# State-space inputs and outputs reordered through DRAM, and one GELU operation per chunk, in a hybrid decoder block

## The chip, the cores and the metric

The program runs on one core of a Trainium2 chip. A core has a matrix engine (TensorE, PE in the profile, its weight loads PEld), a vector engine (VectorE, DVE), a scalar engine (ScalarE, ACT), GpSimd (POOL) and a synchronisation engine (SyncE, SP), which in the kernel before issues all transfers. Each engine works off its own instructions in order. The metric is device time in microseconds of one execution, lower is better.

## The reference, cut to what matters

One decoder layer on 512 tokens of width 1024 in float32: a conditioned norm, one input projection, two parallel token mixers (attention, and a state-space branch called S5), their gated merge, and a mixture of 32 experts. The change touches the S5 branch only:

```python
ug = u.reshape(B, S, 32, 16)                    # 512 columns = 32 groups of 16 channels
bu_re = einsum('bsgh,gph->bsgp', ug, bb_re)     # 64 states a group; bu_im alike
xr, xi = associative_scan(...)                  # x[t] = a * x[t-1] + bu[t], complex, along 512 tokens
y = einsum(xr, c_re) - einsum(xi, c_im) + d_skip * ug
y = gelu(y)                                     # then y @ w_glu, split, sigmoid gate
```

## The kernel before, in words

Weights come in 52 units of 512 KB (ws, four buffers). Of each, ACT makes a rounded copy wh (line 153) and VectorE the remainder wl (line 90), and PE multiplies three products (hh by wh, hl by wh, hh by wl; line 180, for v line 185). The input projection first makes u and two of the q blocks in six PSUM banks (line 543, acc), then the other q and the k blocks (acc), v (vps), and gates. Beside it PE computes the conditioning vector from 32 units adaw (line 749, mvb), which have two, later four buffers.

The S5 branch is worked in four chunks c of 128 channels and is interleaved with that projection: `tick` (line 788) advances a generator, `ssm_steps` (line 704). The scan is taken four tokens at a time. So the tokens t = 4b + q of a chunk, channels 32j + h, are brought into a tile U (us in the profile) whose partitions are 32q + h, with free dimensions j and b, in `ssm_u`: sixteen ACT copies of 32 partitions by 128 elements, with a step of 4 tokens on the reading side (line 420). They read u from PSUM for chunk 0, and for the others from a copy of u in SBUF (line 574). Then, for each chunk: `ssm_in` makes the input matrices W by PE transposes (bt, line 428) and ACT copies (line 429); `ssm_rotate` multiplies (bu, line 652) and VectorE rotates with cos and sin tables (m, z); `ssm_scan` scans; `ssm_back` rotates back (xri); `ssm_y` multiplies into one PSUM bank yp (lines 692 and 694), whose partitions are 32p + h, tokens t = 4b + p. Sixteen ACT operations apply the GELU and put each piece of 32x128 into its place in yf, with a step of 4 tokens on the writing side (line 698). ACT rounds yf to ygh and VectorE makes the rest, ygl; both are read much later, by the GLU. The table of chunk c + 1 (`table`, lines 409 to 411) needs two ACT table loads around it, since the GELU and the sine are in different sets.

The order of each engine's instructions in this part is chosen when the kernel is built, by the framework's scheduler with its own time line; only the first projection (lines 519 to 564) is in the order written. PSUM bank 4 holds yp of one chunk at a time, banks 2 and 3 hold bt and bu, U has two buffers, and yf has two (tag hf).

SP waits in order for what a transfer needs (a free buffer, the data, and a free one of eight completion counters taken in turn); what is queued behind it waits too.

Of the kernel before, what the change touches and what calls it, by code (L numbers as in the profile page):

```python
# [9 lines left out]
F32 = mybir.dt.float32  # L10
# [3 lines left out]
AF = mybir.ActivationFunctionType  # L14
OP = mybir.AluOpType
# [4 lines left out]
T, D = 512, 1024  # L20
# [37 lines left out]
def hybrid_block(ctx: ExitStack, tc: tile.TileContext, x, cols, cst, ada_a, ada_b, b_rows, bc_rows, lamv, relb,  # L58
                 onehot, units, rw, rb, bpad, cpad, w_ein, w_eout, out):
    nc = tc.nc  # L60
    V, S, G, TE = nc.vector, nc.scalar, nc.gpsimd, nc.tensor
# [3 lines left out]
    dram = ctx.enter_context(tc.tile_pool(name="dram", bufs=1, space=DRAM))  # L65

    def bank(i, shape=(128, 512), name=None):
        return psum.tile(list(shape), F32, tag=f"b{i}", name=name or f"bank{i}")
# [3 lines left out]
    late = p1.enter_context(tc.tile_pool(name="late", bufs=1))  # L72
# [4 lines left out]
    def t1(tag, shape, dt=F32, name=None):  # L77
        pool = late if tag[:-1] == "tmp" else mid if tag[:-1] in ("BT", "CT", "sgA", "xs") else early
        return pool.tile(list(shape), dt, tag=tag, name=name or tag)
# [3 lines left out]
    def emit(o, f):  # L83

        if kept[0] is None:
            return f()
        kept[0].append((0.1 + math.prod(o.shape[1:]) / 960, f))

    def tt(o, a, b, op, eng=None):
        return emit(o, lambda: (eng or V).tensor_tensor(o, a, b, op=op))  # L90
# [21 lines left out]
    def f32(a):  # L112
        return a.bitcast(F32)
# [82 lines left out]
    def two(i, name):  # L196
        if i == 0:
            return [bank(0, name=name), bank(1, name=name)]
        t = pair(name=name)
        return [t[:, 0], t[:, 1]]  # L200
# [114 lines left out]
    v, y, t = (st4[:, j] for j in range(3))  # L315
# [97 lines left out]
    U, W = {}, {}  # L413

    def ssm_u(c):

        U[c] = t1(f"v{c % 2}", [128, 4, 128], name="us")
        for j in range(4):
            for q in range(4):
                S.copy(U[c][32 * q:32 * q + 32, j], uT[c][32 * j:32 * j + 32, q::4])  # L420

    def ssm_w(c, ps):

# [95 lines left out]
    with tc.manual_schedule(engines={mybir.EngineType.PE, mybir.EngineType.DVE, mybir.EngineType.Activation}):  # L519
# [4 lines left out]
        acc = two(0, "acc0") + two(1, "acc2") + [bank(m, name=f"acc{m}") for m in (4, 5)]  # L524
# [11 lines left out]
        for k in range(KC):  # L536
            first, second = unit_parts(UNITS[k]) if k in UNITS else (lambda: None, ) * 2
            for n in range(3 * 6):

                m, w = (n // 2, n % 2) if n < 12 else (n - 12, 2)  # L540
                b = 6 * k + m
# [26 lines left out]
    for _ in setup:  # L568
        pass

    uT = [acc[0]]
    for c in range(1, 4):
        uT.append(t1(f"u{c}", [128, T]))
        S.copy(uT[c], acc[c])
        if c == 1:
            ssm_u(0)
    qT, kT, vt = [None] * 4, [None] * 4, [None] * 4

# [57 lines left out]
    ygh, ygl = [None] * 4, [None] * 4  # L636
# [3 lines left out]
    def ssm_in(c):  # L640
        if c:
            ssm_u(c)
            ps = pair((128, 2, 4, 128), "bt")
            ssm_w(c, [ps[:, ri] for ri in range(2)])
# [43 lines left out]
    def ssm_y(c, x_):  # L688
        yp = bank(4, (128, 4, 128), "yp")
        for j in range(4):  # L690
            for ri in range(2):
                TE.matmul(yp[:, j], CA[c // 2][ri][:, 4 * (c % 2) + j].rearrange("p q h -> p (q h)"), x_[:, ri, j], start=ri == 0,
                          stop=False)
            TE.matmul(yp[:, j], G_[c][:, j].rearrange("p q h -> p (q h)"), U[c][:, j], start=False, stop=True)
        f = late.tile([128, T], F32, tag="hf", bufs=2, name="yf")
        for j in range(4):
            for p in range(4):
                S.activation(f[32 * j:32 * j + 32, p::4], yp[32 * p:32 * p + 32, j], AF.Gelu_apprx_tanh)  # L698
        ygh[c] = t1(f"u{c}", [128, T], F32R, name=f"ygh{c}")
        ygl[c] = t1(f"cos{c}", [128, T], F32R, name=f"ygl{c}")  # L700
        S.copy(ygh[c], f)
        tt(ygl[c], f, f32(ygh[c]), OP.subtract)

    def ssm_steps():

        z, x_ = None, None
        for c in range(4):
            z = ssm_rotate(c)
            if c + 1 < 4:
                ssm_in(c + 1)  # L710
            yield
            ssm_scan(c, z)
            yield
            if c:
                ssm_y(c - 1, x_)
                bias_load(c - 1)
                yield
            x_ = ssm_back(c, z)
            yield
            if c == 0:  # L720
                for p in range(4):
                    for half in range(2):
                        powers(CA[half], c0, "c", p + 1, p, half, tx[1])
                        yield
                for half in range(2):
                    setup_g(c0, half)
                    yield
            if c + 1 < 4:
                table(c + 1)
                yield  # L730
        ssm_y(3, x_)
        bias_load(3)
        yield
# [236 lines left out]
    for i in range(4):  # L970
        m2s = []
        for m in (2 * i, 2 * i + 1):
# [5 lines left out]
            a = t1(f"u{m % 2}", [128, T], name="ma")  # L978
            b = t1(f"u{2 + m % 2}", [128, T], name="mb")
# [5 lines left out]
        for j in range(2):  # L985
            cs = slice(256 * i + 128 * j, 256 * i + 128 * j + 128)
            v = m2s[j].rearrange("p (i t) -> p i t", t=128)
# [238 lines left out]
    with tc.manual_schedule(engines={mybir.EngineType.PE}):  # L1226
# [10 lines left out]
        for i in range(NT):  # L1237
            ps = bank((5, 0, 1, 0)[i], name="po2")
            n = T if i < 3 else 256
            for s_ in range(KC * T // n):  # L1240
                k, c0 = s_ % KC, n * (s_ // KC)
# [19 lines left out]
    def slot(name, n=None, t=F32):  # L1261
        if n is None:
            n = nring[0] = nring[0] + 1
        return p2r.tile([128, 2, D], t, tag=f"r{FREED[n % RING]}", name=name)
# [110 lines left out]
    def act(hid):  # L1375
        a = p2.tile([128, 512], F32, tag="hT", name="sa")
        S.activation(a, hid[0], AF.Silu)  # L1377
        tt(a, a, hid[1], OP.mult)
        return a
# [94 lines left out]
    for p in range(NP - 1):  # L1474
# [7 lines left out]
        a = act(hid)  # L1482
# [65 lines left out]
    a = slot("sa", free[0] + 3)[:, 0, :512]  # L1548
# [265 lines left out]
```

## Time and profile before

| | |
|---|---|
| median of 3 runs | 939.51 us (938.96 to 942.91) |
| profiled execution | 938.94 us, span 937.1 us |
| PE busy | 893.2 us (95%) |
| DVE busy | 502.0 us (54%) |
| ACT busy | 300.3 us (32%) |
| transfers | 268.70 MB, mean 287 GB/s |

The span runs from the first to the last instruction of the profiled execution. A busy share is a mean over the whole span: the S5 branch lies between about 60 and 207 us, the attention part up to about 310, the merge, output projection and routing up to about 450, the experts after that. Waits are put down to the instruction that came last before the waiting one could start. PEclk is the granted clock of PE: 1.00 is 2.4 GHz, 0.50 is 1.2 GHz.

### The profile page before, as it was taken

Reading aid. Unit: us, or ns where it says so; the run is one execution under the profiler, and the core shown is the slowest. Engines: PE = TensorE matmul, PEld = TensorE weight load, DVE = VectorE, ACT = ScalarE, POOL = GpSimd, SP = SyncE. Lnnn points to the kernel's source line nnn. Section 1 sums busy time; section 2 is a strip of 40 time slices with the busy share of each in tenths; the row PEclk is TensorE's granted clock in tenths of the full one; section 3 lists DMA queues with packets and bytes.
Section 4 is the critical chain, followed back from the end, with each engine's and each line's share of the span. In section 5 each row is a group of like instructions: output and inputs, shape, how many; then the busy total and the mean of one; then the engine's idle time right before and its main releaser. Section 6 shows DMA issues by size and latency. Waiting matters only on the chain.

```text
span 937.1 us, 12889 instructions
## 1 busy us (share of the span) xinstructions
PE 893.2 (95%) x4967; PEld 554.4 (59%) x4967; DVE 502.0 (54%) x1256; ACT 300.3 (32%) x616; POOL 2.2 (0%) x8
## 2 busy tenths in 40 slices
PE   8997997889999999999999999999999999999994
PEld 4775765567778788778455543555435554355343
DVE  7896685656765557469524432544225442244336
ACT  4565568895644433243201000010000100001014
POOL 0000000000000000000000000000000000000000
PEclk9998999999999999999999999999999999999998
DMA  9925765612222623691899999999999999999952
GB/s 362 376 82 175 253 219 194 218 55 86 68 68 69 220 94 126 262 376 40 343 379 417 420 420 420 420 420 420 420 420 420 420 420 419 420 420 420 419 174 93
DMA packets 77590, 268.70 MB, mean 287 GB/s; under 512 B 5535, under 2 KB 11567, under 8 KB 77524
## 3 DMA queue, kind: packets, MB, share of 16 engines
q1 hardware_dynamic: 77524, 267.82, 72.9%
q8 instruction: 41, 0.67, 0.3%
q14 instruction: 25, 0.20, 0.1%
HBM read 265.68 MB, written 3.17 MB: 287 GB/s over the span
## 4 chain that ended last, share of the span: by engine, by line
PE 83%; ACT 6%; DVE 6%; DMA 3%; issue 1%; SPq 0%; DVEq 0%; ACTq 0%
PE hid L1412 23%; PE yb L1419 11%; PE acc L180 11%; PE cb L1397 7%; PE xg L1155 6%; PE pAS L180 5%; PE po L185 4%; PE acc L543 4%; DMA adaw<-ada_b 3%; ACT us L420 3%; PE plg L180 2%; ACT yf L698 2%; PE pv L864 1%; PE lp L1088 1%; PE mv L474 1%
## 5 line engine op out<-in xcount | busy, mean ns | idle before, releaser
L1412 PE MATMUL hid<-w,xT 128*64 128x512 f32 x1024 | 222.9, 592 | 0.0
L1412 PEld LDWEIGHTS hid<-w,xT 128*64 128x64 f32 x1024 | 73.3, 137 | 145.3 <-issue 136.5
L1419 PE MATMUL yb<-w,sa 128*64 128x512 f32 x480 | 106.3, 595 | 0.0
L90 DVE TENSOR_TENSOR sa<-sa,hid 128x512 f32<-128x512 f32 (+1 forms) x17 | 11.1, 656 | 166.3 <-PE hid L1412 153.9
L90 DVE TENSOR_TENSOR wl<-ws,wh 128x1024 fp32r<-128x1024 f32 x52 | 63.5, 1223 | 56.1 <-ACT wh L153 45.4
L90 DVE TENSOR_TENSOR x<-x,cb 128x512 f32<-128x512 f32 (+1 forms) x132 | 79.9, 664 | 2.0 <-PE cb L1397 2.0
L153 ACT ACTIVATE wh<-ws 128x1024 fp32r<-128x1024 f32 x51 | 53.7, 1057 | 80.0 <-PE acc L180 24.5
L180 PE MATMUL acc<-hh,wh 128*128 128x512 f32 x176 | 74.1, 421 | 4.4 <-ACT wh L153 4.4
L1390 ACT CAST yh<-yf 128x512 fp32r<-128x512 f32 x29 | 17.9, 619 | 172.0 <-DVE yf L96 141.7
L1419 PEld LDWEIGHTS yb<-w,sa 128*64 128x64 f32 x480 | 33.2, 137 | 65.0 <-issue 64.4
L180 PE MATMUL acc<-hl,wh 128*128 128x512 f32 x176 | 70.9, 403 | 0.0
L180 PE MATMUL acc<-hh,wl 128*128 128x512 f32 x176 | 70.6, 402 | 0.0
L1377 ACT ACTIVATE sa<-hid 128x512 f32<-128x512 f32 x15 | 9.0, 597 | 177.0 <-PE hid L1412 177.0
L96 DVE SCALAR_TENSOR_TENSOR yf<-yb,ws,gate 128x512 f32<-128x512 f32 x29 | 21.8, 751 | 80.8 <-PE yb L1419 80.3
L1155 PE MATMUL xg<-P,mh 128*128 128x256 f32 x224 | 54.7, 284 | 0.0
L1155 PE MATMUL xg<-P,ml 128*128 128x256 f32 x224 | 53.5, 280 | 0.0
L1397 PE MATMUL cb<-yh,PT 128*128 128x512 f32 x116 | 48.2, 416 | 0.4 <-ACT yh L1390 0.3
L1397 PE MATMUL cb<-yl,PT 128*128 128x512 f32 x116 | 45.9, 396 | 2.1 <-DVE yl L90 2.0
L1155 PEld LDWEIGHTS xg<-P,ml 128*128 128x128 f32 x224 | 42.2, 189 | 0.5
L1155 PEld LDWEIGHTS xg<-P,mh 128*128 128x128 f32 x224 | 42.1, 188 | 0.5
L180 PEld LDWEIGHTS acc<-hh,wh 128*128 128x128 f32 x176 | 33.7, 191 | 14.1 <-ACT wh L153 4.6
L180 PEld LDWEIGHTS acc<-hh,wl 128*128 128x128 f32 x176 | 33.5, 190 | 9.4 <-issue 1.6
(316 smaller groups left out, 1441.3 us busy)
## 6 DMA issues: line engine op xcount, KB each, us to landing
w<-w_ein SPq DMA_DIRECT2D x128, 1024.0 KB, 13.3
w<-w_eout SPq DMA_DIRECT2D x63, 1024.0 KB, 17.5
ws<-units SPq DMA_DIRECT2D x52, 512.0 KB, 3.6
adaw<-ada_b SPq DMA_DIRECT2D x32, 512.0 KB, 4.5
ada<-ada_a SPq DMA_DIRECT2D x8, 512.0 KB, 8.2
ada<-ada_a SPq DMA_DIRECT2D x16, 256.0 KB, 7.1
X<-x SPq DMA_DIRECT2D x4, 512.0 KB, 6.4
x<-x SPq DMA_DIRECT2D x4, 512.0 KB, 5.5
```

Of the source, the lines that this page charges most:

```text
L90: return emit(o, lambda: (eng or V).tensor_tensor(o, a, b, op=op))
L96: return emit(o, lambda: V.scalar_tensor_tensor(o, a, s, b, op0=op0, op1=op1, **k))
L153: return (lambda: S.activation(hi, st, AF.Copy) if u else V.tensor_copy(hi, st)), lambda: tt(lo, st, f32(hi), OP.subtract)
L180: TE.matmul(o, a, b, start=start and i == 0, stop=stop and i == 2)
L185: TE.matmul(o, a, b, start=start and i == 0, stop=stop and i == 2)
L420: S.copy(U[c][32 * q:32 * q + 32, j], uT[c][32 * j:32 * j + 32, q::4])
L543: TE.matmul(acc[m], (hi, lo, hi)[w], hT(k)[w // 2], start=k == 0 and n < 12 and w == 0, stop=k == KC - 1 and w == 2)
L698: S.activation(f[32 * j:32 * j + 32, p::4], yp[32 * p:32 * p + 32, j], AF.Gelu_apprx_tanh)
L1155: TE.matmul(o, (h2h, h2l)[w][i][:, 128 * k:128 * k + 128], P[:, i].rearrange("p a b -> p (a b)"), start=start, stop=i == NT - 1 and w == 1 ...
L1397: TE.matmul(ps, PT if len(y) == 2 else f32(PT), a, start=w == 0, stop=w == len(y) - 1)
L1412: m = TE.matmul(hid[q][64 * e:64 * e + 64], xT[p, k // 4][:, k % 4, 64 * e:64 * e + 64], ring[p][k][:, e, 512 * q:512 * q + 512], start=k ...
L1419: TE.matmul(yb[q][64 * e:64 * e + 64], hT_[:, f, 64 * e:64 * e + 64], ring[p][8 + f][:, e, 512 * q:512 * q + 512], start=f == 0, stop=f == ...
```

## The change

The reordering of u and of y is taken from ACT's small copies and given to transfers. For u, ACT copies a chunk from PSUM in one operation, with the tokens regrouped by q, and writes it to a DRAM tile ud from its own queue; four transfers from SP's queue read it back into U, one for each q, 64 KB each. For y, one GELU of 128x512 writes yf, a transfer from ACT's queue writes it to a DRAM tile yd, and four transfers on SP's queue read it into a second yf tile. The rounding cast and the subtraction then read that tile with a step of 128 elements between neighbouring tokens.

```diff
--- before.py
+++ after.py
@@ -415,9 +415,9 @@
     def ssm_u(c):
 
         U[c] = t1(f"v{c % 2}", [128, 4, 128], name="us")
-        for j in range(4):
-            for q in range(4):
-                S.copy(U[c][32 * q:32 * q + 32, j], uT[c][32 * j:32 * j + 32, q::4])
+        v = ud[c].rearrange("(j h) (q b) -> q h j b", h=32, b=128)
+        for q in range(4):
+            nc.sync.dma_start(U[c][32 * q:32 * q + 32], v[q])
 
     def ssm_w(c, ps):
 
@@ -568,11 +568,13 @@
     for _ in setup:
         pass
 
-    uT = [acc[0]]
-    for c in range(1, 4):
-        uT.append(t1(f"u{c}", [128, T]))
-        S.copy(uT[c], acc[c])
-        if c == 1:
+    ud = []
+    for c in range(4):
+        u_ = t1(f"u{c}", [128, T], name="u")
+        S.copy(u_.rearrange("p (q b) -> p q b", q=4), acc[c].rearrange("p (b q) -> p q b", q=4))
+        ud.append(dram.tile([128, T], F32, name=f"ud{c}"))
+        nc.scalar.dma_start(ud[c], u_)
+        if c == 0:
             ssm_u(0)
     qT, kT, vt = [None] * 4, [None] * 4, [None] * 4
 
@@ -693,13 +695,19 @@
                           stop=False)
             TE.matmul(yp[:, j], G_[c][:, j].rearrange("p q h -> p (q h)"), U[c][:, j], start=False, stop=True)
         f = late.tile([128, T], F32, tag="hf", bufs=2, name="yf")
+        S.activation(f, yp.rearrange("p j b -> p (j b)"), AF.Gelu_apprx_tanh)
+        yd = dram.tile([128, T], F32, name=f"yd{c}")
+        nc.scalar.dma_start(yd, f)
+        f = late.tile([128, T], F32, tag="hf", bufs=2, name="yf")
+        v = yd.rearrange("(p h) (j b) -> j h p b", h=32, b=128)
         for j in range(4):
-            for p in range(4):
-                S.activation(f[32 * j:32 * j + 32, p::4], yp[32 * p:32 * p + 32, j], AF.Gelu_apprx_tanh)
+            nc.sync.dma_start(f[32 * j:32 * j + 32].rearrange("h (p b) -> h p b", p=4), v[j])
         ygh[c] = t1(f"u{c}", [128, T], F32R, name=f"ygh{c}")
         ygl[c] = t1(f"cos{c}", [128, T], F32R, name=f"ygl{c}")
-        S.copy(ygh[c], f)
-        tt(ygl[c], f, f32(ygh[c]), OP.subtract)
+        f, yh, yl = (a.rearrange(o, **k) for a, o, k in ((f, "h (p b) -> h b p", dict(p=4)), (ygh[c], "h (b p) -> h b p", dict(p=4)),
+                                                         (ygl[c], "h (b p) -> h b p", dict(p=4))))
+        S.copy(yh, f)
+        tt(yl, f, f32(yh), OP.subtract)
 
     def ssm_steps():
```

The scheduler orders the instructions anew. On ACT, after the first projection (u copies and q copies, `us` is U, `lmt` a scalar of the attention, `tv` a bias table), before:

```order
L420 COPY us<-acc_281 32x128 x4
L574 COPY u_866<-acc_282 128x512
L420 COPY us<-acc_281 32x128 x12
L574 COPY u_885<-acc_283 128x512
L574 COPY u_887<-acc_283 128x512
L581 ACTIVATE q_889<-acc_284 128x512
L581 ACTIVATE q_891<-acc_285 128x512
L420 COPY us<-u_866 32x128 x6
L768 COPY tv<-tvp 4x320
L420 COPY us<-u_866 32x128 x10
L919 ACT_TABLE_LOAD
L919 ACTIVATE lmt<-lmt 128x2
```

The same place after the change:

```order
L574 COPY u<-acc_281 128x512
L574 COPY u<-acc_282 128x512
L576 DMA ud_868<-u 128x512
L576 DMA ud_877<-u 128x512
L574 COPY u<-acc_283 128x512 x2
L583 ACTIVATE q_887<-acc_284 128x512
L583 ACTIVATE q_889<-acc_285 128x512
L576 DMA ud_881<-u 128x512
L576 DMA ud_885<-u 128x512
L776 COPY tv<-tvp 4x320
L927 ACT_TABLE_LOAD
L927 ACTIVATE lmt<-lmt 128x2
```

The 32 small copies of chunks 0 and 1 are gone from in front of tv and lmt; four whole copies and four DMA issues stand there.

On SP, at the weight loads ws that follow the first projection, before:

```order
L747 DMA adaw<-ada_b 128x1024 x2
L145 DMA ws_917<-units 128x1024
L145 DMA ws_1027<-units 128x1024
L770 DMA tvd<-tv 4x640
L747 DMA adaw<-ada_b 128x1024 x2
L145 DMA ws_1110<-units 128x1024
```

The same place after:

```order
L755 DMA adaw<-ada_b 128x1024 x2
L420 DMA us<-ud_868 32x4x128 x4
L420 DMA us<-ud_877 32x4x128 x4
L145 DMA ws_915<-units 128x1024
L145 DMA ws_1013<-units 128x1024
L778 DMA tvd<-tv 4x640
L755 DMA adaw<-ada_b 128x1024 x2
L145 DMA ws_1096<-units 128x1024
```

Eight reads of us for chunks 0 and 1 now stand between the adaw loads and the two ws loads; each group of four waits for a write from ACT's queue.

On ACT, around the GELU of chunk 0 (`sin` and `tabtmp` belong to the next chunk's table), before:

```order
L420 COPY us<-u_885 32x128 x16
L698 ACT_TABLE_LOAD
L698 ACTIVATE yf<-yp 32x128 x16
L153 ACTIVATE wh_1847<-ws_1845 128x1024
L409 ACT_TABLE_LOAD
L409 ACTIVATE sin_1650<-tabtmp 128x512
L701 CAST ygh_1590<-yf 128x512
L410 ACTIVATE tabtmp<-tabtmp 128x512
```

And after:

```order
L429 COPY W<-bt 128x512 x2
L698 ACT_TABLE_LOAD
L698 ACTIVATE yf<-yp 128x512
L700 DMA yd_1549<-yf 128x512
L153 ACTIVATE wh_1793<-ws_1791 128x1024
L409 ACT_TABLE_LOAD
L409 ACTIVATE sin_1616<-tabtmp 128x512
L410 ACTIVATE tabtmp<-tabtmp 128x512
L709 CAST ygh_1556<-yf 128x512
L411 ACTIVATE cos_1615<-tabtmp,halfpi 128x512
```

The copies of us for chunk 2 are gone, the GELU is one operation with a DMA issue behind it, and the cast ygh has moved behind the table's second operation.

On SP, where chunk 2 is read and chunk 0 comes back, after (before, there are none of these reads):

```order
L755 DMA adaw<-ada_b 128x1024
L420 DMA us<-ud_881 32x4x128 x3
L755 DMA adaw<-ada_b 128x1024
L420 DMA us<-ud_881 32x4x128
L704 DMA yf<-yd_1549 32x4x128 x4
L145 DMA ws_2106<-units 128x1024
L755 DMA adaw<-ada_b 128x1024
L763 DMA mrd<-mr 4x256
```

The reads of us for chunk 2 and of yf for chunk 0 stand among the adaw loads, ahead of the next ws.

## Rows read from the trace of the kernel before

**Rows 1.** Table of stretches, core 0: us, busy us of each engine, PEclk, DMA share, GB/s.

```profile
75.50:86.10 10.60, 4.93 (x24) 2.73 (x21) 7.92 (x16) 5.83 (x10) 0.00 (x0) 0.68 0.46 162
86.10:143.20 57.10, 54.13 (x348) 39.79 (x347) 44.22 (x83) 32.92 (x70) 0.00 (x0) 1.00 0.69 238
143.20:156.80 13.60, 8.46 (x75) 6.10 (x73) 6.62 (x10) 10.52 (x20) 0.00 (x0) 1.00 0.38 120
156.80:174.30 17.50, 13.39 (x85) 9.34 (x83) 10.78 (x17) 16.78 (x37) 0.00 (x0) 0.92 0.65 237
182.60:198.20 15.60, 12.39 (x87) 8.18 (x85) 11.91 (x19) 14.89 (x31) 0.00 (x0) 1.00 0.43 167
207.00:310.00 103.00, 103.00 (x506) 81.73 (x505) 65.49 (x218) 54.52 (x125) 0.00 (x0) 1.00 0.23 73
500.00:880.00 380.00, 380.00 (x1965) 185.83 (x1964) 143.99 (x279) 34.10 (x66) 0.00 (x0) 1.00 1.03 420
```

**Rows 2.** List of waits, PE, 60 to 210 us: us in total, times, longest us.

```profile
PE acc L180 <- ACT wh L153: 4.4, 1, 4.4
PE bu L652 <- ACT W L429: 4.1, 1, 4.1
PE bt L428 <- DVE m L90: 3.6, 2, 2.3
PE sc L837 <- DVE qs L90: 3.2, 2, 2.8
PE mvb L749 <- DMA adaw<-ada_b: 2.9, 3, 1.5
PE yp L692 <- ACT yf L698: 1.6, 1, 1.6
PE mvb L749 <- DVE mr L90: 1.3, 1, 1.3
```

**Rows 3.** Instructions in order of time, ACT: start us, us, line, operation, count.

```profile
72.30 4.30 ACT L420 COPY us<-u 32x128 f32<-32x128 f32 x10
76.62 1.28 ACT L919 ACT_TABLE_LOAD   x1
...
78.81 2.00 ACT L153 ACTIVATE wh<-ws 128x1024 fp32r<-128x1024 f32 x2
...
132.94 6.93 ACT L420 COPY us<-u 32x128 f32<-32x128 f32 x16 [0.53 <-PE yp L694]
```

**Rows 4.** Instructions in order of time, PE, then DVE (its own view): wait in brackets.

```profile
79.91 0.79 PE L180 MATMUL acc<-hh,wh 128*128 128x512 f32 x1 [4.36 <-ACT wh L153]
...
78.15 0.16 DVE L96 SCALAR_TENSOR_TENSOR lmt<-lmt 128x1 f32<-128x1 f32 x1 [7.22 <-ACT lmt L919]
```

**Rows 5.** Groups of instructions by shape, ACT, 60 to 330 us: busy, mean ns, idle before.

```profile
L698 ACT ACTIVATE yf<-yp 32x128 f32<-32x128 f32 x64 | 25.1, 392 | 3.1 <-PE yp L694 2.4
...
L633 ACT ACTIVATE th<-acc 128x512 f32<-128x512 f32 x16 | 9.3, 580 | 0.0
```

**Rows 6.** Line 420: ns min/median/max, first and last start us, shape.

```profile
L420 ACT COPY us<-u x48: 408/418/447, 69.3 to 163.6; 32x128 f32<-32x128 f32 x48
L420 ACT COPY us<-acc x16: 252/256/260, 62.5 to 67.1; 32x128 f32<-32x128 f32 x16
```

**Rows 7.** Line 145 (weight loads): ns min/median/max of an issue; then issue to landing.

```profile
L145 SPq DMA_DIRECT2D ws<-units x52: 327/328/5805, 4.3 to 383.8; - x52
...
DMA to landing us min/median/max: 3.4/3.6/17.9
```

**Rows 8.** Transfer issues by line: count, KB each, median us from issue to landing.

```profile
adaw<-ada_b SPq DMA_DIRECT2D x32, 512.0 KB, 4.5
...
out<-fo SPq DMA_DIRECT2D x4, 512.0 KB, 2.6
...
B<-bsd SPq DMA_DIRECT2D x4, 256.0 KB, 3.8
...
colt<-cols SPq DMA_DIRECT2D x1, 107.5 KB, 2.0
```


## Prediction

> **What bounds the kernel now.** I read the table of stretches first. In its last two rows [rows 1] TensorE (PE) is busy all the time at a granted clock of 1.00, in the attention part (207 to 310 us) and in the expert part (500 to 880 us); the expert part also keeps the transfers full at 420 GB/s. So nothing is to be won there, and a microsecond won earlier reaches the end only if the expert weights start earlier too (a rival below). The lost time lies between 75 and 198 us, where PE's busy time is clearly below the stretch: 10.60 − 4.93 = 5.7 us idle in the first row, 13.60 − 8.46 = 5.1 in the third, 17.50 − 13.39 = 4.1 in the fourth, 15.60 − 12.39 = 3.2 in the fifth, and 57.10 − 54.13 = 3.0 spread over the long second one [rows 1]. After a wait PE also runs at the lower clock level: the first stretch has a mean of 0.68, so two thirds of it passed at 1.2 GHz, and about half of its 4.9 us of work, 2.5 us, is lost to that. The fourth has 0.92, 16% of 17.5 us at the low level, which costs 1.4 us.
>
> Then the list of waits says whom PE waits for [rows 2]: ScalarE's weight copy wh (4.4), its copy W (4.1) and its GELU yf (1.6); VectorE's m (3.6), mr (1.3) and qs (3.2); a transfer of adaw (2.9). ScalarE (ACT) is the root of more of it than its own rows. Its in-order timeline [rows 3] shows why: ten copies of us run from 72.30 for 4.30 us, and only at 78.81 come the two wh. PE's row of 79.91 has waited 4.36 us for the first of them [rows 4], since 75.5. VectorE sits behind the same queue: its row of 78.15 has waited 7.22 us for ACT's lmt [rows 4]. At 132.94 sixteen copies for chunk 2 take 6.93 us [rows 3], and the GELU of a chunk follows them. By group, ACT spends 25.1 us on 64 GELU pieces (6.3 a chunk) [rows 5], and on 64 copies 48 × 0.42 + 16 × 0.256 = 24.3 us [rows 6], 49.4 us in all.
>
> **The change part by part.** *Removed:* 64 copies and 64 GELU pieces, 49.4 us of ACT. *Added on ACT:* four whole GELUs of 128x512. The trace has none of that shape; a tanh of that shape from PSUM took 580 ns [rows 5], so 4 × 0.6. One more whole copy of u (0.6; three were there already). Eight transfer issues, which the trace shows on SP's queue only, at 0.33 us undisturbed [rows 7], so 8 × 0.33 = 2.6. ACT is relieved of about 44 us, some 11 per chunk.
>
> *The first wait (75.5 to 86.1).* u and the two q copies now come first on ACT, and lmt and wh stand right behind them, so ACT is ready for wh from about 72. What decides is when its weights arrive: the two loads ws now stand on SP's queue behind eight reads of us, and those behind ACT's writes. My reckoning: ACT starts on u at 62.5, as the first copy from acc did [rows 6]; six whole operations of 0.6 and four issues of 0.33 later, at 67.4, the last write is issued, and a write lands 2.6 us after its issue (the nearest row is the output of 512 KB [rows 8]), so 70.0. The first load goes out behind it near 70.2 (SP's order, and it takes over the completion counter of that write), lands 3.6 us later [rows 7], 74, and the cast (2.00 us for two [rows 3]) is ready at 75. PE wants it at 75.5. The second is ready about 1 us later. VectorE, free of its 7.22 us wait, has the other operand by 76.5. So the idle 5.7 and the clock loss 2.5 go, and I charge 0.5 for the tie: −7.7. Bounds: −8.2 if the loads land sooner; −4 if they land 4 us later, as a 256 KB read took 3.8 where I take 2.0 [rows 8].
>
> By the Trainium skill, *DMA: Bandwidth & Descriptors*, section "Issuing engines are not separate DMA queues", ACT's transfers run on the same 16 engines as SP's and interleave with them. The trace before cannot show it: all its program transfers are SP's. By that rule the four writes, 1 MB, would delay the two loads by 1 MB over 420 GB/s [rows 1], 2.5 us, and the sum would be about 2 us higher, inside my range.
>
> *The stretches 143.2 to 156.8 and 156.8 to 174.3.* Their idle 5.1 and 4.1 us, and 1.4 us of clock, come from PE waiting for yf, W, m and mr, each of which stands behind ACT's 13 us of pieces. After the change the yp bank is free 0.6 us after its last matmul, W and the weight copies follow at once, and us arrives by transfer while PE still multiplies v. What is late next is ACT's cast ygh, which now waits for the GELU's round trip: issue 0.33, write 2.6, four read issues 1.3, landing 2.0 (the nearest row, 107.5 KB alone [rows 8]) to 3.8, together 6.2 to 8.0 us. Ahead of that cast stand wh (1.0, half of 2.00), a table load (1.28 [rows 3]), sin and abs (0.58 each, as the tanh), 3.4 us, so ACT holds for 3 to 4.5 us. It saved about 12 in that chunk (6.9 + 6.3 − 0.6 − 0.3); behind the cast wait cos and the next wh, which PE needs a unit of v later, 24 passes of about 0.2 us (506 in 103 us [rows 1]). I cost the hold at nothing, hidden by that unit; if the cover is gone it costs up to 4.5 for each of chunks 0 and 1, 9 in all. The casts of chunks 2 and 3 stand behind work of the attention part. The sum takes −10.6 (5.1 + 4.1 + 1.4).
>
> *The rest.* The 3.2 us wait for qs hangs on VectorE's own chain of chunk 3, which keeps its length: 0, between −3.2 and +4 (if PE arrives ahead of VectorE). The 2.9 us for adaw stay, and a faster PE comes nearer to loads that need 4.5 us [rows 8] and are issued only when PE has freed their buffer: +0.5, between −2.9 and +6. The cast and the subtraction now read f with a stride. A small copy from PSUM takes 256 ns, from u in SBUF 418 [rows 6]; if all of that is the stride, it is 1.3 ns an element, 0.65 us on each of eight operations, beside work of other engines: 0, at most +5.
>
> Sum: −7.7 − 10.6 + 0.5 = −17.8 us. The profiled execution took 938.94 us, 0.6 below the median of 939.51, so 921.1 on its own scale; I predict **921 us**.
>
> **The rivals.** *A, only the first wait goes.* The holds at ygh and SP's queue (the reads of us wait there for PE's yp, those of yf for the write, with adaw and ws behind them) put back what the later stretches gave. For it: SP issues in order, and one load here took 17.9 us to land and 5.8 to issue behind a large transfer [rows 7]. Against it: the reads stand where SP waited for PE before too. 938.9 − 7.7 = **931 us**.
>
> *B, slower.* One mechanism: the read of yf back from DRAM gets stuck behind the adaw loads, ACT stops at ygh, and wh behind it starves PE. It decides once the round trip exceeds what ACT saved plus what stands ahead: 12 + 3.4 = 15.4 us. If landing takes the worst row, 17.9 us [rows 7], the round trip is 0.33 + 2.6 + 1.3 + 17.9 = 22.1, 6.7 us beyond that point. Chunks 0 and 1 then cost 13.4 us more than before instead of giving 10.6, while the first wait still goes: 938.9 − 7.7 + 13.4 = 944.6, **945 us**. Against it: that 17.9 stood behind a 1 MB transfer that is made once.
>
> *C, no change at the end.* The time is won but the expert weights do not start earlier, and with transfers full at 420 GB/s [rows 1] PE waits there instead: **939 us**. For it: share 1.03 from 500 to 880. Against it: PE is busy 380 of 380 us there, so the loads keep up, and they start when earlier buffers come free, which moves with PE.
>
> *D, it does not do what it says:* the whole GELU or the casts cost so much more that ACT is not relieved. With 44 us to lose I give it no time of its own and count it with C.
>
> **How the numbers follow.** Forecast 0.74, A 0.14, B 0.07, C with D 0.05. The forecast's own range is 914 to 929: at the low end all idle time of 75 to 198 us goes (5.7 + 3.0 + 5.1 + 4.1 + 3.2 = 21.1) and both clock losses (3.9), 938.9 − 25.0; at the high end the first wait gives only 4 and adaw takes 4 more than charged: 921.1 + 3.7 + 4. The range of 8 in 10 goes on to A, and below by 3 us, since gaps between matmuls too short to show as idle may close as well: 911 to 932. About 0.5% (4.7 us) is what a measurement of this kernel can tell from no change. Faster by more than that: 0.74 + 0.14 = 0.88; the same, C and D: 0.05; slower, B: 0.07.
>
> **What would show it.** Right: PE's row of the first weight pass after gp has no wait over 1 us; no row of PE waits for yf; VectorE no longer waits 7 us for lmt; the first score matmul, whose wait for qs ended at about 197 us before, starts between 175 and 183; everything from there on keeps its length. ACT's wait ahead of each ygh is 3 to 5 us, and its weight casts behind do not stand at the head of PE's waits. Wrong: the wait for wh stays with a transfer of ws as the releaser; PE waits for wh behind ygh; adaw heads PE's waits with over 8 us; or the expert part grows by what was won.

## The result and the profile after

The changed kernel took 926.99 us (median of 4 runs, 923.54 to 928.20), the kernel before in the same series 940.28 (938.96 to 942.91): ratio 0.9849, 95% interval 0.9814 to 0.9884. That is 13.3 us faster, where 18 were forecast: inside the range, 6 us from its likeliest value. The profiled execution took 926.62 us, its span is 924.8, where it was 937.1.

I cut both traces at the same points of the work. The *front* runs from the last matmul of the first projection to the first matmul of v (line 185). The *middle* runs from there to the first score matmul (line 837 before, 845 after). First the table of stretches of the kernel before (columns as in [rows 1]): front, middle, and a stretch behind the first score matmul:

```profile
63.59:120.94 57.35, 50.75 (x334) 36.60 (x335) 42.13 (x89) 32.92 (x71) 0.00 (x0) 0.94 0.62 215
120.94:197.03 76.09, 61.94 (x444) 43.55 (x442) 53.29 (x91) 64.57 (x132) 0.00 (x0) 0.98 0.55 196
198.80:202.30 3.50, 3.50 (x10) 2.75 (x9) 2.02 (x8) 3.40 (x9) 0.00 (x0) 0.51 0.44 150
```

And of the kernel after: front, in it the place of the first wait, middle, attention, and a part of the experts that is as long as the last row of [rows 1]:

```profile
64.61:120.98 56.37, 53.63 (x345) 37.59 (x345) 45.02 (x96) 24.17 (x46) 0.00 (x0) 0.94 0.80 271
76.95:86.40 9.45, 6.71 (x23) 3.95 (x23) 8.84 (x13) 3.17 (x3) 0.00 (x0) 0.65 0.68 239
120.98:186.56 65.58, 61.02 (x434) 43.49 (x432) 53.78 (x85) 34.39 (x51) 0.00 (x0) 0.97 0.73 240
186.56:298.00 111.44, 111.44 (x545) 88.44 (x544) 69.41 (x230) 59.29 (x133) 0.00 (x0) 1.00 0.25 78
488.00:868.00 380.00, 380.00 (x1964) 185.81 (x1964) 143.94 (x280) 33.96 (x66) 0.00 (x0) 1.00 1.03 420
```

The first length on a row tells it. The front is 57.35 before and 56.37 after: it gave 1.0 us. The middle is 76.09 and 65.58: it gave 10.5, of which 9.6 is idle time of PE (76.09 − 61.94 = 14.15 before, 65.58 − 61.02 = 4.56 after); the other 0.9 is work that moved, since eight adaw matmuls and two small ones now stand ahead of the first v matmul. From the first score matmul to the end it was 937.1 − 197.03 = 740.1 and is 924.8 − 186.56 = 738.2, another 1.8. Nearly all of that is the lower clock behind the wait for qs (0.51 in the third row, 1.7 us lost), which the kernel after does not have there. Against this stands 1.0 us ahead of the front (63.59 to 64.61), where the clock from 15 to 20 us is 0.67, and 1.00 before. Each engine does the same operations in both programs there, and of the kernels below some show the lower clock and some do not. Together −12.3, the difference of the spans. Attention and experts run as before: PE busy throughout at a clock of 1.00, the experts' transfers at 420 GB/s.

The list of waits of PE, 60 to 210 us, answers to [rows 2]:

```profile
PE mvb L757 <- DMA adaw<-ada_b: 3.1, 3, 1.3
PE yp L694 <- DVE xri L90: 2.5, 1, 2.5
PE acc L180 <- ACT wh L153: 1.7, 2, 1.2
```

The waits for yf, W, m, mr and qs are gone. The wait for wh, 4.4 us before, is 1.7 and did not go, and a new one, for xri of the last chunk, takes the place of the one for qs. ACT's groups by shape, 60 to 330 us, answer to [rows 5]:

```profile
L709 ACT CAST ygh<-yf 128x512 fp32r<-128x512 f32 x4 | 4.4, 1100 | 3.8 <-DMA yf<-yd 3.8
...
L698 ACT ACTIVATE yf<-yp 128x512 f32<-128x512 f32 x4 | 2.4, 600 | 5.6 <-PE yp L696 5.6
```

A whole GELU takes 600 ns, four of them 2.4 us in place of 25.1.

The first wait is read in order of time. SP's issues (start, length, line, transfer, count), first the two weight loads before the change, then the same place after it:

```profile
65.12 0.84 SPq L145 DMA_DIRECT2D ws<-units  x2
```

```profile
65.24 0.83 SPq L755 DMA_DIRECT2D adaw<-ada_b  x2
66.20 6.80 SPq L420 DMA_DIRECT2D us<-ud  x8
73.10 0.85 SPq L145 DMA_DIRECT2D ws<-units  x2
```

ACT, in order of time, at that place and around the first two round trips of y (the write yd, and the cast that waits for its reads):

```profile
77.04 1.06 ACT L153 ACTIVATE wh<-ws 128x1024 fp32r<-128x1024 f32 x1 [3.92 <-DMA ws<-units]
78.28 1.06 ACT L153 ACTIVATE wh<-ws 128x1024 fp32r<-128x1024 f32 x1 [0.19 <-DMA ws<-units]
...
132.73 0.33 ACTq L700 DMA_DIRECT2D yd<-yf  x1
...
141.66 1.09 ACT L709 CAST ygh<-yf 128x512 fp32r<-128x512 f32 x1 [3.21 <-DMA yf<-yd]
...
150.03 0.33 ACTq L700 DMA_DIRECT2D yd<-yf  x1
...
164.62 1.09 ACT L709 CAST ygh<-yf 128x512 fp32r<-128x512 f32 x1 [0.58 <-DMA yf<-yd]
```

Eight reads keep SP for 6.8 us; the two weight loads behind them leave at 73.10, ACT now waits for them instead of they for ACT, and PE, ready at 76.95, waits 1.18 and 0.52 us:

```profile
78.14 0.50 PE L180 MATMUL acc<-hh,wh 128*128 128x512 f32 x1 [1.18 <-ACT wh L153]
...
79.39 0.50 PE L180 MATMUL acc<-hh,wh 128*128 128x512 f32 x1 [0.52 <-ACT wh L153]
```

The round trip of chunk 0 is 132.73 to 141.66, 8.9 us. That of chunk 1 is longer, 150.03 to 164.62, 14.6 us, but other work and waits of ACT cover all of it but 0.58.

### The profile page after: what moved, and what is told of

Read it like the earlier page. It is cut to its first block, busy times and chain, and to the rows that moved or that the text cites. A ratio compares the mean times of both kernels' runs of the same rounds, so it can differ in the third digit from the quotient of the medians.

```text
span 924.8 us, 12835 instructions
## 1 busy us (share of the span) xinstructions
PE 895.0 (97%) x4967; PEld 554.8 (60%) x4967; DVE 504.1 (55%) x1256; ACT 256.5 (28%) x493; POOL 2.2 (0%) x8
## 4 chain that ended last, share of the span: by engine, by line
PE 86%; DVE 7%; DMA 4%; ACT 1%; issue 1%; SPq 0%; DVEq 0%; ACTq 0%
PE hid L1420 24%; PE acc L180 13%; PE yb L1427 11%; PE cb L1405 7%; PE xg L1163 6%; PE pAS L180 5%; PE po L185 4%; PE acc L543 3%; PE plg L180 2%; DMA adaw<-ada_b 1%; DMA yd<-yf 1%; PE pv L872 1%; PE lp L1096 1%; PE mv L474 1%; PE mvb L757 1%
## 5 line engine op out<-in xcount | busy, mean ns | idle before, releaser
L90 DVE TENSOR_TENSOR sa<-sa,hid 128x512 f32<-128x512 f32 (+1 forms) x17 | 11.1, 657 | 166.3 <-PE hid L1420 153.9
```

## The experiments

All times are medians of 4 to 6 runs against the kernel before in the same series; an interval of a ratio is ±0.2 to 0.35%, 2 to 3 us. So only differences above some 4 us can be told by the times, and the traces decide on mechanisms. A trace is of one execution, and that is not always a middling one: for u alone through SP it took 925.4 us (median 927.4), for y alone 928.7 (932.9), for the first SP experiment 930.5 (928.2), and for the two kernels without the hold 934.6 (930.0) and 929.8 (927.0). In the tables, "idle" is a stretch less PE's busy time, "clock" the sum over half-microsecond pieces of busy time × (1 − granted clock).

My first theory (T): ACT's relief is the gain, and the front gave its share back because SP issues in order. Rivals: the gain is the GELU's alone (G); the transfers, not the order, made the weights late (B).

**One part alone.** First the u part with the 16 GELU pieces a chunk kept (the main lines of the edit, seen from the changed kernel):

```diff
-        S.activation(f, yp.rearrange("p j b -> p (j b)"), AF.Gelu_apprx_tanh)
...
+                S.activation(f[32 * j:32 * j + 32, p::4], yp[32 * p:32 * p + 32, j], AF.Gelu_apprx_tanh)
```

> The u part of the change alone: us by transfers through DRAM, the GELU of a chunk in 16 pieces as before and no y transfers. ScalarE loses 24 us of copies and keeps 25 us of pieces. Theory T (what pays is ScalarE's relief in the stretch from 121 us to the first score matmul, which came 10.5 us earlier, and either half of the relief empties most of the queue): ratio to before about 0.991, 931 to 933 us; TensorE's wait for W (4.1 before) under 1 us, its wait for yf near 1 to 2 us again, first score matmul near 190. Rival G (the gain is the GELU's alone): 937 to 941 us.

Then the y part with the 64 copies kept (the copy of u from PSUM goes back to the old form as well):

```diff
-        for q in range(4):
-            nc.sync.dma_start(U[c][32 * q:32 * q + 32], v[q])
+        for j in range(4):
+            for q in range(4):
+                S.copy(U[c][32 * q:32 * q + 32, j], uT[c][32 * j:32 * j + 32, q::4])
```

> The y part of the change alone: one GELU per chunk and its way through DRAM, us by 64 copies on ScalarE as before. Theory T: the first wait is as long as before (4.4 us for wh near 75.5), since the copies stand ahead of it, but that wait was worth only about 2 us net; the later stretch gains most of its 10.5: 930 to 933 us, ratio about 0.991. Rival G (the gain is the GELU's alone): 926 to 928 us. Rival U (the gain is that of the copies alone): 937 to 941 us.

Measured: u alone 927.42 us (0.9874, interval 0.9852 to 0.9896), y alone 932.86 (0.9929, 0.9905 to 0.9952). The second is as T said, and its list of waits of PE has the first wait as before:

```profile
PE acc L180 <- ACT wh L153: 4.4, 1, 4.4
```

The first is 3.6 us below T's range: within what the times can tell, the u part alone gives all that the whole change gives. Its front, and its middle:

```profile
63.47:118.36 54.89, 52.59 (x345) 36.96 (x345) 44.83 (x96) 24.14 (x46) 0.00 (x0) 0.97 0.81 280
118.36:181.90 63.54, 58.76 (x433) 41.66 (x432) 49.25 (x82) 47.69 (x93) 0.00 (x0) 1.00 0.65 220
```

Both are shorter than in the changed kernel (56.4 and 65.6); behind the first score matmul it takes 3.5 us more (741.7 for 738.2), 1.7 of it lost to the lower clock. So in this order of work the y part adds nothing to the u part. G falls, and so does the rival U of the second text, by which y alone would have given nothing.

**SP's queue.** The reads of us issued by GpSimd, and, in another kernel, two weight loads (of the units 7 and 8) asked for earlier:

```diff
-            nc.sync.dma_start(U[c][32 * q:32 * q + 32], v[q])
+            nc.gpsimd.dma_start(U[c][32 * q:32 * q + 32], v[q])
```

> The changed kernel with the 16 reads of us issued by GpSimd instead of SyncE; the bytes and the writes are the same. Theory T (the first wait came back because SyncE issues in order and spent 6.8 us on eight reads, 66.20 to 73.10, so that the two weight loads left 8 us later than before): the two loads leave by 67.5, their casts stand at 73 to 74, the waits of 1.18 and 0.52 us at 78 go, and part of the 2.5 us lost at the lower clock with them: 922 to 925.5 us. Rival B (the loads were late because 2 MB of writes and adaw loads were on the same 16 transfer engines): the loads leave earlier but land no earlier than 76, and the time stays at 926 to 928 us. Either way us must be there by 74.3; if GpSimd's issue is slow, TensorE waits for us instead and the time is over 928.

```diff
+    load(7)
+    load(8)
     ud = []
```

> The changed kernel with the loads of weight units 7 and 8 asked for ahead of the copies of u, so that they stand ahead of the eight reads on SyncE. Theory T: no wait for wh at 78; the reads of us come 1 to 2 us later and TensorE, which has weights, multiplies q meanwhile: 922 to 926 us. Rival B: the bytes only change places, us lands 2.5 us later, TensorE waits for bu's operand or VectorE's chain of chunk 0 is late by that: 926 to 930 us.

Measured: 928.20 us (0.9867, 0.9844 to 0.9889) and 929.05 (0.9884, 0.9863 to 0.9905): no gain, and 2.7 and 3.1 us above T's ranges. The second is where B put it, yet without a wait for wh in a front of 53.6 us, as T had it. But it does not test the order alone, since its loads left long before the writes of u, as the last two of four that start at 41.17:

```profile
41.17 8.53 SPq L145 DMA_DIRECT2D ws<-units  x4
```

They were out of the crowded time altogether. The middle of the second is 70.3 us, with 4.7 of PE's waits for xri. The stretches of the first, front and middle, show that T was right on the front's length and blind to what follows:

```profile
64.85:118.05 53.20, 50.38 (x345) 35.96 (x346) 45.05 (x96) 24.38 (x47) 4.46 (x8) 1.00 0.82 287
118.05:189.79 71.74, 64.86 (x434) 45.90 (x432) 53.55 (x85) 34.21 (x50) 4.40 (x8) 0.91 0.69 226
```

The front is 3.2 us shorter than in the changed kernel and never at the lower clock; the middle is 6.2 longer. PE's idle time in the front is as before, 2.8 us for 2.7: the waits for wh went, and PE waits 0.9 us for us and 1.9 for adaw, so the 3.2 us are the clock's. And B was half right. SP's issue of the two loads in that kernel, then ACT's casts of what they bring:

```profile
66.41 1.29 SPq L145 DMA_DIRECT2D ws<-units  x2
```

```profile
75.36 1.06 ACT L153 ACTIVATE wh<-ws 128x1024 fp32r<-128x1024 f32 x1 [2.00 <-DMA ws<-units]
77.74 1.06 ACT L153 ACTIVATE wh<-ws 128x1024 fp32r<-128x1024 f32 x1 [1.33 <-DMA ws<-units]
```

The loads left 6.7 us sooner and the first was there only 1.7 us sooner: 9 us on the way, where 3.6 was the median before [rows 7]. Where the middle lost is in the list of waits of PE:

```profile
PE mvb L757 <- DVE mr L90: 3.4, 1, 3.4
PE yp L694 <- ACT th L635: 3.2, 1, 3.2
```

and on ACT in order of time:

```profile
140.65 1.07 ACT L709 CAST ygh<-yf 128x512 fp32r<-128x512 f32 x1 [9.17 <-DMA yf<-yd]
```

ACT stood 9.2 us at ygh, which the scheduler had put ahead of the table's operations (in the changed kernel it stands behind two of them), and at each of PE's two waits the clock fell to 0.50 for over 5 us. So the second theory (T2): the hold at ygh took the front's gain. Its rival (S): VectorE's chain through the four chunks binds the middle anyway.

**The hold.** Four kernels: the u part with GpSimd's reads (the two edits shown); then the cast reading the GELU's own tile, with GpSimd's reads and with SP's (these two leave out the reordering of y and serve for the time alone); then the whole GELU for chunks 2 and 3 only (`if c >= 2:` around the new y lines, the pieces otherwise), with GpSimd's reads.

> The u part alone (as in the first experiment, 927.4 us) with the reads of us issued by GpSimd (as in the third). Theory T2 (two separate things: SyncE's eight reads cost the front 3 us, which GpSimd's issue gives back; and the y transfers through DRAM, not the u part, took that gain away again by holding ScalarE 9.2 us at ygh): front from the end of the first projection to the first v matmul 53 to 54 us instead of 54.9, first score matmul 1 to 3 us sooner than 181.9, 924 to 926 us, ratio 0.983 to 0.985. Rival S (the later stretch is bound by VectorE's chain of the four chunks, whatever the front gains): first score matmul within 1 us of 181.9 and 926.5 to 928.5 us.

```diff
+        f_ = f
         f = late.tile([128, T], F32, tag="hf", bufs=2, name="yf")
...
-        f, yh, yl = (a.rearrange(o, **k) for a, o, k in ((f, "h (p b) -> h b p", dict(p=4)), (ygh[c], ...
+        f, yh, yl = (a.rearrange(o, **k) for a, o, k in ((f_, "h (p b) -> h b p", dict(p=4)), (ygh[c], ...
```

> The whole change with the reads of us on GpSimd (928.2 us), and the casts ygh and ygl read the GELU's own tile instead of the one read back; all transfers stay, so only ScalarE's and VectorE's waits for the round trip go (y then stands in the wrong order, which changes the output). Theory T2: the 9.2 us hold at ygh goes, with it VectorE's 7.2 us behind it, TensorE's 3.4 us for mr and 3.2 us for th, and the stretch from the first v matmul to the first score matmul falls from 71.7 to 63 to 66 us: 921 to 924 us. Rival S (VectorE's chain or adaw loads bind it anyway): the stretch stays over 69 us, 926 to 928.5 us.

> The changed kernel (927.0 us) with the casts reading the GELU's own tile, transfers unchanged (y in the wrong order). It prices the hold that the prediction costed at nothing: ScalarE waited 3.2 and 0.6 us at ygh of chunks 0 and 1 and no TensorE wait stood behind it. Theory T2: within 1.5 us of the changed kernel, 925.5 to 928.5. Rival (the hold is a hidden price, through VectorE's chain and the 2.5 us wait for xri): 922 to 925 us.

> A candidate that uses both readings: us through DRAM read by GpSimd's queue, the whole GELU and its round trip for chunks 2 and 3 only, whose casts stand behind work of the attention part, and 16 pieces for chunks 0 and 1. Theory T2: no long hold at ygh, 923 to 926 us, within 1.5 us of the u part alone with GpSimd's reads. Rival S: 926.5 to 928.5 us.

Measured: 932.59 us (0.9920, 0.9902 to 0.9938), 930.04 (0.9890, 0.9872 to 0.9907), 927.00 (0.9853, 0.9835 to 0.9871) and 930.41 (0.9895, 0.9877 to 0.9913). The third prices the hold of the changed kernel: nothing that the times can tell. The others sink T2, by 4 us and more above its ranges: with the hold gone, or never there, the middle is 72.3, 73.7 (in the execution of 934.6 us) and 72.2 us. S's figures were too low as well. In all three PE waits 6.1 to 7.2 us for xri of the last chunk; in the u part with GpSimd's reads, PE's own row:

```profile
184.88 0.77 PE L694 MATMUL yp<-xri,CA 128*128 128x128 f32 x2 [6.12 <-DVE xri L90]
```

and what VectorE did until then, in order of time:

```profile
169.32 0.86 DVE L820 CAST qs<-q 64x512 fp32r<-64x512 f32 x2
170.22 1.22 DVE L90 TENSOR_TENSOR wl<-ws,wh 128x1024 fp32r<-128x1024 f32 x1
...
172.68 1.40 DVE L90 TENSOR_TENSOR qs<-q,qs 64x512 fp32r<-64x512 f32 x2
...
182.73 0.69 DVE L90 TENSOR_TENSOR qs<-q,qs 64x512 fp32r<-64x512 f32 x1
183.45 0.69 DVE L90 TENSOR_TENSOR ygl<-yf,ygh 128x512 fp32r<-128x512 f32 x1
184.06 0.68 DVE L90 TENSOR_TENSOR xri<-m 128x508 f32<-128x508 f32 x1
184.66 1.22 DVE L90 TENSOR_TENSOR wl<-ws,wh 128x1024 fp32r<-128x1024 f32 x1
185.79 0.68 DVE L90 TENSOR_TENSOR xri<-m 128x508 f32<-128x508 f32 x1
```

Operand splits of the attention stand ahead of xri, the pair at 169.32 and 172.68 for head 1, which is not needed before the fifth score block. That pair takes 2.3 us; a weight remainder wl, ygl and splits of head 0 stand ahead of xri too. Third theory (V): the order of VectorE's work, made by the scheduler, sets the end of the middle.

**VectorE's order.** In four kernels the splits of head 1 are held behind chunk 3's xri and head 0's splits (`tails` keeps the last of each):

```diff
-                next(splits)
+                with ExitStack() as behind:
+                    for w in tails if t == 1 else ():
+                        behind.enter_context(tc.issue_after(w.ins))
+                    next(splits)
```

> The changed kernel (927.0 us), with the operand splits of attention head 1 (qs and kl, 4.6 us of VectorE) held behind the last xri of chunk 3 and the splits of head 0; nothing else moves. Theory V (what sets the first score matmul after the change is VectorE's order: splits of head 1, not needed before the fifth score block, stand ahead of chunk 3's xri, for which TensorE waits 2.5 us and then runs 3 to 4 us at the lower clock): the wait for xri falls under 0.7 us, first score matmul 2 to 4 us sooner, 923 to 925.5 us. Rival Q (VectorE has as much to do either way, and the wait moves to qs of head 0): within 1.5 us of 927.0.

> The same edit on the kernel whose reads of us are issued by GpSimd (928.2 us; its front is 3 us shorter than that of the changed kernel and its stretch behind it 6 us longer). Theory V: the front's gain now reaches the end: 921 to 924.5 us, stretch from the first v matmul to the first score matmul 66 to 68 us instead of 71.7. Rival Q: 926.5 to 929 us.

> The same edit on the u part alone with GpSimd's reads (932.6 us, TensorE waited 6.1 and 0.9 us for xri). Theory V: those 7 us fall to under 3, 926 to 929 us, ratio 0.985 to 0.988. Rival Q: TensorE waits as long for qs, 931 to 934 us. If bu of chunk 3 itself comes late (VectorE waited 4.4 us for it at 167 us), a wait of 3 to 5 us for xri stays and the time is 929 to 931 us.

> The same edit on the u part alone with SyncE's reads (927.4 us, where xri came in time and TensorE waited 1.2 and 1.1 us for qs of head 0). Theory V: the two waits for qs fall under 0.7 us, 925 to 926.5 us; candidate for the fastest. Rival Q: 926.5 to 928.5 us.

| kernel, with head 1 held | time, ratio (interval) | front: us, idle, clock | middle: us, idle, clock |
|---|---|---|---|
| changed | 923.33, 0.9827 (0.9801 to 0.9853) | 58.4, 5.7, 1.7 | 60.8, 1.8, 0 |
| changed, GpSimd reads | 925.32, 0.9852 (0.9822 to 0.9881) | 52.9, 2.5, 0 | 67.7, 6.6, 1.7 |
| u part, GpSimd reads | 927.32, 0.9873 (0.9848 to 0.9897) | 55.3, 3.5, 1.7 | 65.7, 5.3, 1.4 |
| u part | 931.40, 0.9915 (0.9896 to 0.9934) | 54.8, 2.2, 1.7 | 69.4, 6.7, 4.3 |

V holds for three (the second is 0.8 us over its range): PE's wait at the last chunk's y (2.5 for xri, 3.2 for th and 7.0 for xri without the edit) went, went, and fell to 2.1, and the middle is 4.7, 4.1 and 6.5 us shorter than without the edit (65.58, 71.74 and 72.28). More moved than the edit names: in the first, head 0's casts of q are behind the last xri too, and that xri starts at 178.57 instead of 182.00. So the order is shown to matter, not head 1's splits by themselves. Rival Q, by which the wait moves to qs, falls in these three: no wait for qs is over 0.4 us. The first of them has the best time. Its list of waits of PE, 60 to 200 us, is two rows long:

```profile
PE mvb L759 <- DMA adaw<-ada_b: 5.4, 3, 3.0
PE acc L180 <- ACT wh L153: 2.1, 2, 1.5
```

The interval of its ratio overlaps that of the changed kernel, so I call it faster by the trace (a middle of 60.8 for 65.6) and not by the times. The last kernel missed: 4 us slower than without the edit. PE's row, and ACT in order of time:

```profile
183.96 1.22 PE L696 MATMUL yp<-xri,CA 128*128 128x128 f32 x4 [3.68 <-ACT yf L702]
```

```profile
173.72 0.62 ACT L826 CAST kd<-kT 64x512 fp32r<-64x512 f32 x1 [4.75 <-DVE m L90]
...
176.23 1.28 ACT L702 ACT_TABLE_LOAD   x1
177.53 6.39 ACT L702 ACTIVATE yf<-yp 32x128 f32<-32x128 f32 x16
```

With xri in time the 16 pieces are what is late. The scheduler put four casts kd ahead of them, ACT stood idle 4.75 us for the first of these, and the yp bank is free only after 6.39 us of GELU. Without the edit the pieces of that chunk stood ahead of the casts:

```profile
170.11 6.55 ACT L700 ACTIVATE yf<-yp 32x128 f32<-32x128 f32 x16 [2.07 <-PE yp L696]
```

Between these two orders the y part is worth 931.4 − 923.3 = 8 us, where between the unedited ones it was worth nothing.

## Why the prediction was right in the sum and wrong in a term

*The first wait, −7.7: mis-sized; the front gave 1.0.* The step that failed is "The first load goes out behind it near 70.2": it left at 73.10. From there it went as taken, 3.9 us to the cast for 3.6, and the one write of u whose landing is on record took 2.5 for 2.6. The step charged the eight reads nothing on SP's queue; they held it 6.8 us, and each was taken to land in 2.0, as if alone. SP's transfers of line 420 after the change, issue to landing (min, median, max):

```profile
DMA to landing us min/median/max: 1.9/5.9/6.9
```

Of the 6.8 us, 3.75 are the eight issues (0.30 to 0.83 each, where 0.33 was undisturbed [rows 7]). For 2.7 SP stood until two earlier adaw loads were in, whose completion counters the fifth and the sixth read take. The stretches from 66 to 72 us say what the rest was:

```profile
66.00:68.00 2.00, 2.00 (x9) 1.51 (x9) 2.00 (x9) 1.98 (x5) 0.00 (x0) 1.00 0.98 202
68.00:70.00 2.00, 2.00 (x10) 1.60 (x9) 2.00 (x8) 0.78 (x2) 0.00 (x0) 1.00 0.95 346
70.00:72.00 2.00, 2.00 (x10) 1.35 (x9) 1.90 (x8) 0.01 (x1) 0.00 (x0) 1.00 1.03 381
```

The transfer engines were full (0.95 to 1.03), with four writes of 256 KB, two adaw loads of 512 KB and the reads. The first SP experiment parted the two causes: of the 6.7 us by which the loads left sooner, the way took back 5, on transfer engines shared with other bytes. The Trainium skill, *DMA: Bandwidth & Descriptors*, "Issuing engines are not separate DMA queues", says that transfers of all issuers share the same 16 engines; the trace agrees, with these 5 us, more than the 2 by which the prediction weighed it.

The other half of the term was the clock. PE's idle in the front did fall from 6.6 to 2.7 us, but behind waits of 1.18 and 0.52 us came the lower clock level (0.50, that is 1.2 GHz, from 80 to 86.5 us, with a third wait of 1.04 in it). It lasted as long as the one beside the wait of 4.36: 2.9 us lost, 2.5 before. In both SP experiments, without these waits for wh, the front had none of it and was 53 us. But the waits alone do not decide: with head 1 held, waits of 1.50, 0.59 and 0.59 stand at the same place, and the clock is full:

```profile
76.40:87.00 10.60, 7.93 (x37) 4.97 (x37) 9.86 (x15) 3.65 (x4) 0.00 (x0) 1.00 0.70 252
```

So why the clock fell in the changed kernel stays open. The idle gain of 3.9 less 0.4 of clock and 0.9 for the ten matmuls that now stand ahead of the mark would leave a front 2.6 shorter; the other 1.6 I can't place.

*The middle, −10.6: right in the idle time, and in the sum by luck.* W, yf, m and mr no longer hold PE: 9.6 us where 9.2 was taken. The 1.4 of clock did not come (1.7 us lost before, 1.6 after, now beside the wait for xri); the 0.9 of work that moved to the front, which is no gain, makes the sum 10.5. The hold at ygh, costed at nothing, was 3.2 and 0.6 us on ACT, with VectorE waiting 8.4 us for the two casts, and cost nothing that the times can tell: 927.00 without it. The round trips were 8.9 and 14.6 us, not 6.2 to 8.0: the write yd of chunk 0 landed in 5.2 us and not in 2.6. With GpSimd's reads the hold was 9.2 us and stood behind PE's wait of 3.4 for mr, which went when the hold was taken out: the mechanism of rival B exists, short of its price, and sets in before a round trip of 15.4 us (there it was 129.57 to 140.65, 11.1).

*ACT relieved of 44 us: right* (300.3 us busy before, 256.5 after, though busy time leaves out the eight issues, which the prediction had counted). *But I treated relief as gain.* Alone the two parts give 12.5 and 7.0 us, together 13.3: either half takes away most of PE's waits on ACT, and what is left (adaw, VectorE's operands) the second half does not shorten.

*qs at 0, adaw at +0.5: right in the sum.* The wait for qs (3.2) became one for xri (2.5), adaw went from 2.9 to 3.1. I had left VectorE's chain at its length without asking what stands in front of its last link; by the trace there lay another 4.7 us of the middle. *The strided cast and subtraction* cost 0.49 us on ACT (1100 ns, 607 before) and 0.39 on VectorE (1082, 688 before) where 0.65 was taken; no run prices them at the end.

*The signs I had named:* no PE wait for yf, no 7 us of VectorE for lmt, experts unchanged: right. No wait over 1 us at the first weight pass, and the first score matmul between 175 and 183: wrong, 1.18 and 186.56, by what the front did not give and the 1.0 us ahead of it. A wait of 3 to 5 us ahead of each ygh: 3.2 once, then 0.6. One sign of being wrong came in part: the wait for wh stayed, 1.7 of 4.4 us, its cast released by a transfer of ws. Rival A's doubt about SP's queue was the right one, at the wrong place. C and D did not come.

What stays open, besides the clock: whether more runs would part the changed kernel from the one with head 1 held (0.9849 and 0.9827), and what a kernel with both the short front (53 us) and the short middle (61 us) would take; none here had both.

## What to carry to other kernels

Relief of a busy engine is worth only what its waiters lose before the next limit; look at what stands ahead of their other operands first, order included. Transfers that replace copies must be charged where they run: on the issuing queue (here 6.8 us for eight small reads) and on engines shared with the loads behind them, not at the landing time of one alone. And where the scheduler orders anew, compare the whole order: edits in one place moved work in others here (ygh, xri, the casts kd). Time at the lower clock is no sure gain either: here it stayed whole (2.5 and 2.9 us) when the wait beside it shrank.

## What was not expected of the hardware

Small waits can cost as much clock as a long one, and can cost none: behind waits of 1.18 and 0.52 us the clock was halved for 6.5 us, as long as beside one of 4.36, and beside 1.50, 0.59 and 0.59 at the same place it stayed full. Writes of the same 256 KB from ACT landed in 2.5 us (ud) and in 5.2 (yd, with adaw loads about). Between 66 and 68 us the transfer engines were 0.98 busy at 202 GB/s, half of the 420 that the expert loads reach at 1.03; what ran then were the writes of u, reads in rows of 512 bytes and two adaw loads, and no run parts which of them is slow.
